# A hybrid encoder block on one core: the SwiGLU down projection as seven products behind all gate and up blocks

## The chip, the cores and the metric

The kernel runs on one core of a Trainium2 chip. The engines named below are TensorE (PE; its weight loads are shown apart as PEld), VectorE (DVE), ScalarE (ACT), GpSimd (POOL) and SyncE (SP, which only issues transfers here). The metric is the device time of one execution in microseconds, as the median over several executions.

## The reference

One layer is applied to a prompt of 256 tokens and a sample of 512 tokens, 768 tokens together, with a model width of 1024. It holds an RMSNorm, a joint input projection, three token mixers (a bidirectional state-space scan, a differential attention, an attention into 256 memory tokens), a gated merge with an output projection, and a SwiGLU FFN. The change concerns the FFN, whose hidden width D_FF is 2816. All arrays are float32.

```python
D_FF = -(-8 * D_MODEL // (3 * 256)) * 256
...
    merged = jnp.sum(gates * br.astype(F32), axis=2).astype(x.dtype)
    x = x + merged @ w_out[li]

    h2 = rmsnorm(x, ffn_norm_g[li])
    g, up = jnp.split(h2 @ w_gate_up[li], 2, axis=-1)
    x = x + (jax.nn.silu(g) * up) @ w_down[li]
    return x
```

## The kernel before

**Products in three passes.** A float32 product is made of three matmuls on float32r parts: each operand is split into a high part (a ScalarE copy that rounds) and a low part (the difference, on VectorE, or by an adding transfer on POOL's queue). `mm3` issues high x high, high x low, low x high into one PSUM tile. `split_evac` makes such a pair.

**Weights.** `WStream` holds a list of weight blocks, filled by `W.add` in the order of use. A block is loaded in two halves of 128 x 1024 from SP's queue into the pool "wr" (3 buffers), and split into "wh" and "wl" (4 buffers of 128 x 1024 each, line 544). `W.get` hands out the next block and starts the one behind it (`ahead`, line 605). A block of kind "w" is cut into seven factors of 128 x 512: three are quarters of the block (wh_A, wl_A), the others come from sums and differences that POOL makes in the pool "ws" (line 563 on). A block of kind "x" takes its first half from two extra tiles, so that it rotates with the others.

**The FFN.** The 2816 hidden features are 11 blocks of 256. The normed input lies in F, features on partitions, as a high and a low part of 128 x 8 x 768. Block 0 is computed plainly: `first` makes one gate or up tile of 128 features and 256 or 512 tokens from 24 matmuls. For blocks 1 to 10 gate and up are each a product by Strassen's scheme in Winograd's form: `block` (line 1453) cuts the weights, the features and the tokens in halves and makes seven products of 12 matmuls (128 x 384), where the plain one takes eight. The right factors are quarters B11 to B22 of F and T1 to T4, sums of them, which `right_factors` makes once on VectorE and ScalarE, in steps that end with a `yield`; T4 overwrites B12. The code runs these steps between the tiles of block 0 by calls of `next(factors)`. Within `block`, `plus` adds the products up in two tiles of the pool "brr" (2 buffers), and `fin_gate` (tanh on ScalarE, then VectorE) and `fin_up` (a multiply on POOL) put the result into `act_in`, 128 x 2 x 768. `fin_up` then splits it into hidh (ScalarE) and hidl (VectorE).

**Down.** `down(fb)` (line 1487) takes block fb's 256 hidden features at once: for each of six token tiles and two halves of the 1024 output columns, six matmuls of 128 x 512 go into a PSUM tile, and VectorE adds it into the residual `x1`. The last call also stores the outputs. The order is written by hand (line 720): gate 0, up 0, down 0, gate 1, up 1, and then gate fb, down fb - 1, up fb.

**Who sets the order.** The program is put in order by a scheduler that simulates the engines' times; within an engine or a queue it then runs in that order. So the order of the code is a priority, and an instruction whose inputs or buffers are free sooner can go ahead of one that stands before it in the code. Tiles in pools are reused when their last reader is done.

**Memory around the FFN.** Before the FFN, three branches are projected. In `tail` (line 1552), ahead of the last quarter of the first branch, the pools of the differential attention are closed, their memory becomes XB (48 KB a partition), and eight chunks of z are loaded from DRAM on POOL's queue and split into the pair Z that the next product reads. Four of the chunks go through "zst" (3 buffers), the others through "brr". XB later holds F.

Of the kernel before, what the change touches and what calls it, by code (L numbers as in the profile page):

```python
# [486 lines left out]
TOK = 768  # L487
# [16 lines left out]
class WStream:  # L504
# [7 lines left out]
    def __init__(self, nc, tc, ctx):  # L512
        self.nc = nc
        self.praw = ctx.enter_context(tc.tile_pool(name="wraw", bufs=3))
        self.ph = ctx.enter_context(tc.tile_pool(name="whi", bufs=4))
        self.pl = ctx.enter_context(tc.tile_pool(name="wlo", bufs=4))
        self.sub = nc.vector
        self.by_dma = False
        self.extra = None
# [23 lines left out]

    def _tile(self, i, extra=False):
        ph, pl = self.extra if extra else (self.ph, self.pl)
        return (ph.tile([128, self.HALF], F32R, name=f"wh{i}", tag="wh"),
                pl.tile([128, self.HALF], F32R, name=f"wl{i}", tag="wl"))

    def _factor(self, i, key, src):

        if self.half is None:
            t, sl = self._tile(f"{i}_{key}"), slice(0, 512)
# [6 lines left out]
        self.nc.scalar.activation(f(hi), src, AF.Copy)  # L559
        self.nc.vector.tensor_tensor(out=f(lo), in0=src, in1=f(hi).bitcast(F32), op=ALU.subtract)  # L560
        self.parts.setdefault(i, {})[key] = f(hi), f(lo)
# [23 lines left out]
    def _split(self):  # L585
# [3 lines left out]
        if kind == "w":  # L589
            return self._split_w(i, h)  # L590
        hi, lo = self._tile(f"{i}_{h}", kind == "x" and h == 0)
        self.parts.setdefault(i, []).append((hi, lo))
# [36 lines left out]
def hybrid_block(ctx, tc, A, outs, consts):  # L629
# [89 lines left out]
    wd = A["w_down"].rearrange("(k p) c -> p k c", p=128)  # L719
    order = [("gate", 0), ("up", 0), ("down", 0), ("gate", 1), ("up", 1)]  # L720
    for fb in range(2, NFB):
        order += [("gate", fb), ("down", fb - 1), ("up", fb)]
    order.append(("down", NFB - 1))
    for what, fb in order:
        if what == "down":
            W.add(wd[:, 2 * fb : 2 * fb + 2, :], 2, 1024, "x")
        else:
            W.add(cols("w_gate_up", 256 * fb + (DFF if what == "up" else 0)), 8, 256, "w" if fb else None)

# [25 lines left out]

    def mm3(ps, wh, wl, xh, xl, start, stop):
        pe.matmul(ps, wh, xh, start=start, stop=False)  # L757
        pe.matmul(ps, wh, xl, start=False, stop=False)  # L758
        pe.matmul(ps, wl, xh, start=False, stop=stop)  # L759

# [74 lines left out]
    z_scr = [dr.tile([128, TOK], F32, name=f"z_scr{m}") for m in range(8)]  # L835
    gl_scr = [dr.tile([128, TOK], F32, name=f"gl_scr{m}") for m in range(24)]
    br_scr = [dr.tile([128, TOK], F32, name=f"br_scr{m}") for m in range(8)]
    mo_scr = [dr.tile([128, 8, TOK], F32, name=f"mo_scr{w}") for w in "hl"]
# [287 lines left out]

    x1ctx, dctx, wctx = ExitStack(), ExitStack(), ExitStack()
    stg = x1ctx.enter_context(tc.tile_pool(name="stg", bufs=2))
# [287 lines left out]
    HT = TOK // 2  # L1416
    hid = {}
    act_in = {}
# [7 lines left out]
    def fin_up(fb, c, m, cs, eng=v):  # L1426
        hh, hl = hid[fb]
        o = act_in[fb][:, m, cs]
        eng.tensor_tensor(out=o, in0=o, in1=c, op=mul)
        act.activation(hh[:, m, cs], o, AF.Copy, scale=0.5)  # L1430
        v.scalar_tensor_tensor(out=hl[:, m, cs], in0=o, scalar=0.5, in1=hh[:, m, cs].bitcast(F32),
                               op0=mul, op1=sub)

    def new_block(what, fb):
        if what == "gate":
            act_in[fb] = fa.tile([128, 2, TOK], F32, name=uid("fa"), tag="fa")
        else:
            hid[fb] = tuple(fh.tile([128, 2, TOK], F32R, name=uid("hid" + w), tag="hid" + w) for w in "hl")

# [12 lines left out]

    def block(what, fb):

# [17 lines left out]
        kw = {} if what == "gate" else {"eng": gp}  # L1472
        act.activation(c12, prod("A11", "B11"), AF.Copy)
        plus(c11, c12, prod("A12", "B21"))
        fin(fb, c11, 0, h1, **kw)
# [9 lines left out]
        fin(fb, c21, 1, h1, **kw)  # L1485

    def down(fb, last):
        w = W.get()
        x = hid.pop(fb)
        for tt in (3, 4, 5, 0, 1, 2) if fb else range(TILES):  # L1490
            for c0 in (0, 512):
                ps = (psd if c0 else env.psb)("dn")
                dense_tm(ps, w, c0, 512, x, tt, 2)
                o = x1[tt][:, c0 : c0 + 512]
                v.tensor_tensor(out=o, in0=o, in1=ps, op=add)  # L1495
                if last:
                    nc.sync.dma_start(os_[tt][:, c0 : c0 + 512], o)


    with ExitStack() as c5:  # L1500
# [51 lines left out]
        def tail(c):  # L1552
# [3 lines left out]
            dctx.close()  # L1556
            L["XB"] = x1ctx.enter_context(tc.tile_pool(name="XB", bufs=1))
# [3 lines left out]
            xp = x1ctx.enter_context(tc.tile_pool(name="x1", bufs=1))  # L1561
            L["x1"] = [xp.tile([128, 1024], F32, name=f"x1_{t}") for t in range(TILES)]

# [30 lines left out]
        c6 = ctx.enter_context(ExitStack())  # L1594
        fa = c6.enter_context(tc.tile_pool(name="ffa", bufs=1))
        ft_ = c6.enter_context(tc.tile_pool(name="fft", bufs=2))
# [54 lines left out]

    W.extra = tuple(c6.enter_context(tc.tile_pool(name="wx" + w, bufs=1)) for w in "hl")
    W.sums = c6.enter_context(tc.tile_pool(name="wsum", bufs=3))
    tp = c6.enter_context(tc.tile_pool(name="ffT", bufs=1))
    fh = c6.enter_context(tc.tile_pool(name="ffh", bufs=1))

# [4 lines left out]
    def right_factors():  # L1661

        with tc.tile_pool(name="ffb", bufs=1, side="right") as p:
# [29 lines left out]
            b21 = whole(t1, "B21")  # L1693
            v.tensor_tensor(out=b21, in0=b21, in1=t2, op=sub)
            R["T4"] = B["B12"]
            split_evac(*R["T4"], b21)
# [4 lines left out]
    for sg, m in ((0, 0), (0, 1), (1, 0), (1, 1)):  # L1701
        for what in ("gate", "up"):
            if sg or what == "up":
                first(what, sg, m)
                if sg and m + (what == "up"):
                    next(factors)
    down(0, False)
    next(factors)
    next(factors, None)
    for what, fb in order[3:]:  # L1710
        if what == "down":
            down(fb, fb == NFB - 1)
        else:
            block(what, fb)
    c6.close()
    x1ctx.close()

# [42 lines left out]
```

## Time and profile before

| | |
|---|---|
| median of 3 executions | 1789.56 us (1787.43 to 1792.11) |
| span of the profiled execution, first to last instruction | 1787.8 us |
| mean granted TensorE clock | 0.999 |
| PE, PEld, DVE busy | 99%, 91%, 73% |
| ACT, POOL busy | 48%, 15% |
| moved by DMA in the span | 205.25 MB |
| start of the first down matmul, start of the last addition | 1287.8 us, 1783.9 us |

The profile names the execution's span but no other time of it; the table has the executions beside it. A line of a group of instructions reads: line of the kernel, engine, operation, tiles written and read, shape, count, then busy time and mean duration, then the idle time of the engine ahead of the group with what ended it. A line of the timeline begins with the start and the duration in us. Tile names in the FFN: "gate" and "up" are PSUM tiles of the blocks, "dn" those of the down projection, "fs" the sums of `block`, "fa" is `act_in`, "ft" the tanh, "wr" a raw weight, "wh" and "wl" its parts, "ws" POOL's sums.

### The profile page before, as it was taken

The numbers are of one execution on the slowest core, as the hardware profiler recorded it, in microseconds if no ns is written. First come the engines' busy times: TensorE is split into PE (matmuls) and PEld (weight loads), VectorE is DVE, ScalarE is ACT, GpSimd is POOL, SyncE is SP. The second block draws the span as 40 slices with busy tenths as digits, with TensorE's granted clock in tenths as the row PEclk, the third lists the DMA queues.
The fourth block names the chain that finished last, engine by engine and source line by source line (L and its number), as shares of the span: only waits on it lengthen the run. The fifth ranks groups of instructions, "written<-read, shape, count | busy, mean of one in ns | idle before, by whom it ended". The sixth has DMA issues, their size and how long they took to land.

```text
span 1787.8 us, 29382 instructions
## 1 busy us (share of the span) xinstructions
PE 1761.9 (99%) x11293; PEld 1624.4 (91%) x11293; DVE 1301.2 (73%) x2411; ACT 861.7 (48%) x1838; POOL 261.8 (15%) x276
## 2 busy tenths in 40 slices
PE   9999999999999999999989999999999999999999
PEld 8999988999999999999979888888889999999997
DVE  6665659699999589778865545452699777877775
ACT  6444434777676356777756433232333333333331
POOL 0000000000000101011110101000115333333330
PEclk9999999999999999999999999999999999999999
DMA  7223645664656466553862635332312222222221
GB/s 264 72 83 107 133 118 127 160 147 126 157 146 152 122 164 152 112 113 82 188 166 71 219 116 171 115 98 68 83 48 71 72 71 71 71 71 71 71 71 71
DMA packets 193196, 205.25 MB, mean 115 GB/s; under 512 B 56856, under 2 KB 166688, under 8 KB 193056
## 3 DMA queue, kind: packets, MB, share of 16 engines
q1 hardware_dynamic: 173632, 146.74, 28.0%
q0 software_dynamic: 18272, 53.48, 13.6%
q10 hardware_dynamic: 1152, 3.15, 0.5%
q8 instruction: 89, 1.46, 0.3%
q14 instruction: 51, 0.42, 0.1%
HBM read 145.59 MB, written 32.57 MB: 100 GB/s over the span
## 4 chain that ended last, share of the span: by engine, by line
PE 57%; DVE 4%; DMA 2%; issue 1%; ACT 1%; POOL 0%; SPq 0%; DVEq 0%; ACTq 0%; POOLq 0%
PE br L757 4%; PE br L758 4%; PE br L759 4%; PE dn L757 3%; PE dn L758 3%; PE dn L759 3%; PE gate L757 3%; PE gate L759 3%; PE gate L758 3%; PE up L757 3%; PE up L759 3%; PE up L758 3%; PE av L1316 2%; PE qk L758 2%; PE qk L757 2%; PE qk L759 2%
## 5 line engine op out<-in xcount | busy, mean ns | idle before, releaser
L597 ACT ACTIVATE wh<-wr 128x1024 fp32r<-128x1024 f32 x146 | 163.7, 1122 | 106.6 <-PE br L758 27.0
L603 DVE TENSOR_TENSOR wl<-wr,wh 128x1024 fp32r<-128x1024 f32 x104 | 135.2, 1302 | 102.1 <-ACT wh L597 100.3
L757 PE MATMUL gl<-Hhi,wh 128*128 128x256 f32 (+1 forms) x384 | 132.4, 345 | 2.3 <-ACT glt L1119 2.3
L1495 DVE TENSOR_TENSOR x<-x,dn 128x512 f32<-128x512 f32 x132 | 88.7, 684 | 56.5 <-PE dn L759 56.1
L759 PE MATMUL gl<-Hhi,wl 128*128 128x256 f32 (+1 forms) x384 | 129.0, 336 | 0.0
L758 PE MATMUL gl<-Hlo,wh 128*128 128x256 f32 (+1 forms) x384 | 128.7, 335 | 0.0
L757 PE MATMUL qk<-wh,Hhi 128*128 128x256 f32 x384 | 108.1, 281 | 0.7 <-ACT V L1215 0.7
L758 PE MATMUL qk<-wl,Hhi 128*128 128x256 f32 x384 | 108.6, 283 | 0.0
L759 PE MATMUL qk<-wh,Hlo 128*128 128x256 f32 x384 | 107.9, 281 | 0.0
L559 ACT ACTIVATE wh_S<-ws 128x512 fp32r<-128x512 f32 x70 | 41.7, 623 | 130.1 <-PE dn L759 103.5
L757 PE MATMUL dn<-wh,hidh 128*128 128x512 f32 x264 | 102.4, 390 | 1.3 <-DVE x L1495 1.0
L601 POOL DMA_DIRECT2D wl<-wr x42 | 36.8, 876 | 454.0 <-ACT wl L600 430.5
L758 PE MATMUL dn<-wl,hidh 128*128 128x512 f32 x264 | 102.9, 390 | 0.0
L759 PE MATMUL dn<-wh,hidl 128*128 128x512 f32 x264 | 100.8, 390 | 0.0
L757 PEld LDWEIGHTS gl<-Hhi,wh 128*128 128x128 f32 x384 | 72.3, 188 | 9.7 <-ACT glt L1119 2.7
L759 PEld LDWEIGHTS gl<-Hhi,wl 128*128 128x128 f32 x384 | 72.0, 188 | 8.1
L758 PEld LDWEIGHTS gl<-Hlo,wh 128*128 128x128 f32 x384 | 72.2, 188 | 7.2
L1285 DVE TENSOR_REDUCE nm<-sc 128x1 f32<-128x512 f32 (+1 forms) x96 | 56.5, 597 | 28.0 <-PE sc L1280 27.0
L757 PEld LDWEIGHTS qk<-wh,Hhi 128*128 128x128 f32 x384 | 72.4, 188 | 1.6 <-ACT V L1215 0.9
L759 PEld LDWEIGHTS qk<-wh,Hlo 128*128 128x128 f32 x384 | 72.8, 190 | 0.3
L758 PEld LDWEIGHTS qk<-wl,Hhi 128*128 128x128 f32 x384 | 72.2, 188 | 0.6
L1287 ACT ACTIVATE p<-sc,nm 128x512 f32<-128x512 f32 (+1 forms) x96 | 59.1, 619 | 17.0 <-DVE nm L1285 16.6
(466 smaller groups left out, 5927.6 us busy)
## 6 DMA issues: line engine op xcount, KB each, us to landing
wr<-in_w_in_dram SPq DMA_DIRECT2D x48, 512.0 KB, 4.6
wr<-in_w_gate_up_dram SPq DMA_DIRECT2D x44, 512.0 KB, 3.5
wl<-wr POOLq DMA_DIRECT2D x42, 512.0 KB, 5.3
wr<-in_w_branch_dram SPq DMA_DIRECT2D x24, 512.0 KB, 4.2
wr<-in_w_down_dram SPq DMA_DIRECT2D x22, 512.0 KB, 4.2
glr<-gl_scr POOLq DMA_DIRECT2D x24, 384.0 KB, 3.7
wr<-in_w_mem_kv_dram SPq DMA_DIRECT2D x16, 512.0 KB, 3.7
wr<-in_w_in_dram SPq DMA_DIRECT2D x32, 256.0 KB, 4.5
```

What stands on the lines that cost most here:

```text
L559: self.nc.scalar.activation(f(hi), src, AF.Copy)
L597: self.nc.scalar.activation(hi, r, AF.Copy)
L601: self.nc.gpsimd.dma_start(lo, r.bitcast(F32R), accum_op=ALU.add)
L603: self.sub.tensor_tensor(out=lo, in0=r, in1=hi.bitcast(F32), op=ALU.subtract)
L757: pe.matmul(ps, wh, xh, start=start, stop=False)
L758: pe.matmul(ps, wh, xl, start=False, stop=False)
L759: pe.matmul(ps, wl, xh, start=False, stop=stop)
L1285: v.tensor_reduce(out=nm[:, m : m + 1], in_=ps, axis=AX.X, op=ALU.max, negate=True)
L1287: act.activation(pm[:, 0:n], ps, AF.Exp, bias=nm[:, m : m + 1], accum_out=s1s[:, tt : tt + 1] if m == 0 else s2)
L1316: pe.matmul(po[:, 0:128], aT[:, 128 * k : 128 * k + 128], V[:, c0 // 128 + k, 128 * (h % 2) : 128 * (h % 2) + 128], start=(k == 0), stop=( ...
L1495: v.tensor_tensor(out=o, in0=o, in1=ps, op=add)
```

## The change

The down projection isn't done block by block any more. All gate and up blocks run first, gate and up in turns; each finished `act_in` block (no longer split) is stored to a DRAM tensor, `hid_scr`, from SP's queue (`hid_store`). Then the whole product of 768 tokens x 2816 features x 1024 columns is made with tokens, features and columns cut in halves, as seven products of 384 x 1408 x 512 in the same scheme as gate and up (P1, P5, P6, P3, P7, P2, P4 in this order). A product runs over 11 chunks of 128 features in six granules (five of two chunks, one of one); a granule is 18 matmuls of 128 x 512, three token tiles in three PSUM tiles. Products that belong together are summed in PSUM without being read out in between, in two groups of banks ("b" and "d") used in turns; behind every product VectorE adds three PSUM tiles into `x1`, or subtracts them.

The left operands are sums and differences of quarters of the activations, loaded back from DRAM once each (24 loads, on SP) and combined in place on VectorE, then split. The right operands are sums of quarters of `w_down`, made by transfers: a plain load on SP's queue, then an adding one on POOL's queue onto the same tile (P5, P6, P4 on six tiles "ch", P7 on raw buffers). Loads are issued four granules ahead and operands made two ahead. Three granules' activations and weights are fetched in the middle of the last up block (`hook`).

Beside that: `act_in` has two buffers instead of one, the extra weight tiles and the hid tiles go, `x1` is allocated ahead of XB so that XB can be closed after the gate and up blocks, "zst" has two buffers instead of three, and the steps of `right_factors` are called after each up tile and each gate tile but the last pair, with one more `yield`.

```diff
-    order = [("gate", 0), ("up", 0), ("down", 0), ("gate", 1), ("up", 1)]
-    for fb in range(2, NFB):
-        order += [("gate", fb), ("down", fb - 1), ("up", fb)]
-    order.append(("down", NFB - 1))
+    order = [(what, fb) for fb in range(NFB) for what in ("gate", "up")]
...
     def fin_up(fb, c, m, cs, eng=v):
-        hh, hl = hid[fb]
         o = act_in[fb][:, m, cs]
         eng.tensor_tensor(out=o, in0=o, in1=c, op=mul)
-        act.activation(hh[:, m, cs], o, AF.Copy, scale=0.5)
-        v.scalar_tensor_tensor(out=hl[:, m, cs], in0=o, scalar=0.5, in1=hh[:, m, cs].bitcast(F32),
-                               op0=mul, op1=sub)
+
+    def hid_store(fb):
+        nc.sync.dma_start(hid_scr[:, 2 * fb : 2 * fb + 2, :], act_in.pop(fb))
...
-        zst = zctx.enter_context(tc.tile_pool(name="zst", bufs=3, side="right"))
+        zst = zctx.enter_context(tc.tile_pool(name="zst", bufs=2, side="right"))
...
-                if sg and m + (what == "up"):
+                if (sg, m) != (1, 1):
                     next(factors)
-    down(0, False)
-    next(factors)
-    next(factors, None)
-    for what, fb in order[3:]:
-        if what == "down":
-            down(fb, fb == NFB - 1)
+    for _ in factors:
+        pass
+    hid_store(0)
...
+    P1, P5, P6, P3, P7, P2, P4 = range(7)
+    GRAN = [(k, min(2, NFB - k)) for k in range(0, NFB, 2)]
+    NG = len(GRAN)
+    ITEMS = [(p, g) for p in range(7) for g in range(NG)]
+    AHEAD, FETCH = 2, 4
+    EARLY = 3
...
+    def a_load(q, g):
+        k0, n = GRAN[g]
+        r, kh = q
+        early = q == (0, 0) and g < EARLY
+        t = (da_e if early else DP["a"]).tile([128, 2, HT], F32, name=f"da{r}{kh}_{g}")[:, 0:n]
+        nc.sync.dma_start(t, hid_scr[:, NFB * kh + k0 : NFB * kh + k0 + n, HT * r : HT * r + HT])
+        a_raw[q, g] = t
...
+    def w_fetch(i):
...
+        if p in (P5, P6, P4):
+            if p == P5:
+                ch[g] = view(DP["ch"].tile([128, 1024], F32, name=f"dch{g}"))
+                nc.sync.dma_start(ch[g], w_quarter(0, 0, g))
+            t = ch[g]
+            src, acc = None, {P5: (0, 1), P6: (1, 1), P4: (1, 0)}[p]
         else:
-            block(what, fb)
+            t = view(W.praw.tile([128, W.HALF], F32, name=f"dwr{i}", tag="wr"))
+            src, acc = {P1: ((0, 0), None), P3: ((1, 1), None), P7: ((0, 1), (1, 1)), P2: ((1, 0), None)}[p]
+            nc.sync.dma_start(t, w_quarter(*src, g))
+        if acc:
+            gp.dma_start(t, w_quarter(*acc, g), accum_op=add)
+        w_raw[i] = t
...
+    def make(i):
...
+        split_evac(wh, wl, t)
...
+        xh, xl = (da_f.tile([128, 2, HT], F32R, name=uid("dx" + w), tag="dx" + w)[:, 0:n] for w in "hl")
+        split_evac(xh, xl, x, sign)
+        parts[i] = xh, xl, wh, wl
+
+    def down_early():
+        for i in range(FETCH - 1):
+            w_fetch(i)
+        for g in range(EARLY):
+            a_load((0, 0), g)
+        for i in range(AHEAD):
+            make(i)
+
+    for what, fb in order[2:]:
+        block(what, fb, down_early if (what, fb) == order[-1] else None)
+        if what == "up":
+            hid_store(fb)
     c6.close()
+    xbctx.close()
...
+        loads = [((0, 0), g) for g in range(EARLY, NG)]
+        loads += [(q, g) for g in range(NG) for q in ((1, 0), (1, 1))] + [((0, 1), g) for g in range(NG)]
...
+        for _ in range(NG - EARLY):
+            a_load(*loads.pop(0))
+        w_fetch(FETCH - 1)
+        for i, (p, g) in enumerate(ITEMS):
+            for _ in range(3):
+                if loads:
+                    a_load(*loads.pop(0))
+            w_fetch(i + FETCH)
+            make(i + AHEAD)
+            bank = "b" if p in (P1, P6, P7, P4) else "d"
...
+            for t in range(3):
+                c = slice(128 * t, 128 * t + 128)
+                for k in range(n):
+                    mm3(ps[t], xh[:, k, c], xl[:, k, c], wh[:, k], wl[:, k],
+                        g == 0 and k == 0 and p in (P1, P5, P2), g == NG - 1 and k == n - 1, p in (P6, P3, P7, P4))
+            if g == NG - 1:
+                r, f, op = HOME[p]
+                for t in range(3):
+                    o = x1[3 * r + t][:, 512 * f : 512 * f + 512]
+                    v.tensor_tensor(out=o, in0=o, in1=ps[t], op=op)
+                    if p in (P3, P7, P2, P4):
+                        nc.sync.dma_start(os_[3 * r + t][:, 512 * f : 512 * f + 512], o)
```

More of the change, by code (lines that the diff above doesn't have):

```diff
@@ L1451, in first, with block @@
         (fin_gate if what == "gate" else fin_up)(0, ps[:, 0:n], m, slice(c0, c0 + n))
-    def block(what, fb):
+    def block(what, fb, hook=None):
         new_block(what, fb)
@@ new lines, in make @@
+    def make(i):
+        if i >= len(ITEMS):
+            return
+        p, g = ITEMS[i]
+        n = GRAN[g][1]
+        t = w_raw.pop(i)
+        wh, wl = (x.rearrange("p (k c) -> p k c", k=2)[:, 0:n] for x in W.tiles(f"d{i}"))
+        split_evac(wh, wl, t)
+        A_ = lambda r, kh: a_raw[(r, kh), g]
+        tt = lambda o, x, y, op: v.tensor_tensor(out=o, in0=x, in1=y, op=op)
+        sign = 0.5
+        s_ = None if p == P1 else A_(1, 0)
+        if p == P1:
+            x = A_(0, 0)
+        elif p == P5:
+            x = s_
+            tt(x, x, A_(1, 1), sub)
+        elif p == P6:
+            x = s_
+            tt(x, x, A_(0, 0), sub)
+        elif p == P3:
+            x = DP["t"].tile([128, 2, HT], F32, name=uid("ds4"), tag="ds4")[:, 0:n]
+            tt(x, s_, A_(0, 1), add)
+        elif p == P7:
+            x = s_
+            tt(x, x, A_(1, 1), add)
+            sign = -0.5
+        else:
+            x = A_(*((0, 1) if p == P2 else (1, 1)))
+        xh, xl = (da_f.tile([128, 2, HT], F32R, name=uid("dx" + w), tag="dx" + w)[:, 0:n] for w in "hl")
+        split_evac(xh, xl, x, sign)
+        parts[i] = xh, xl, wh, wl
```

80 lines of the change are left out of this document (44 added, 36 removed).

## The prediction

> **What bounds the kernel now.** I read first the page's totals, then the chain that ended last, then the gate, up and down stages of the FFN one by one, then its start, then the transfers.
>
> ```profile
> span 1787.8 us, 29382 instructions
> PE 1761.9 (99%) x11293; PEld 1624.4 (91%) x11293; DVE 1301.2 (73%) x2411; ACT 861.7 (48%) x1838; POOL 261.8 (15%) x276
> 1783.68 0.24 PE dn L759
> 1783.94 0.69 DVE x L1495
> ```
>
> TensorE (PE) is busy 99% of the span, and the chain runs through its down-projection matmuls ("dn") up to the last at 1783.68; one addition and the store follow, 4.1 us to the end. A change in FFN time is therefore a change in TensorE's work or in its waits. There are 11 blocks x 6 token tiles x 2 column halves x 2 chunks x 3 passes = 792 dn matmuls. Their duration of 0.39 us isn't their price, because they overlap. The next rows (start, duration) give the pitch: the first of one down stage, the first behind it, and the first of the gate block after that.
>
> ```profile
> 1371.91 0.39 PE L757 MATMUL dn<-wh,hidh 128*128 128x512 f32 x1
> 1388.27 0.33 PE L757 MATMUL up<-fhi,wh_A 128*128 128x384 f32 x1
> 1402.85 0.33 PE L757 MATMUL gate<-fhi,wh_A 128*128 128x384 f32 x1
> ```
>
> 72 matmuls took 1388.27 - 1371.91 = 16.36 us, so one costs 0.227 us. The 84 of an up block take 1402.85 - 1388.27 = 14.58 us. Stage by stage (columns: window, length, then busy time of PE, weight load, DVE, ACT, POOL with counts, clock, DMA share, GB/s):
>
> ```profile
> 1357.40:1371.90 14.50, 14.50 (x85) 14.50 (x84) 14.19 (x20) 6.70 (x12) 8.43 (x6) 1.00 0.32 97
> 1371.90:1388.30 16.40, 16.40 (x74) 13.55 (x74) 11.69 (x18) 1.74 (x4) 4.78 (x3) 1.00 0.03 11
> ```
>
> TensorE doesn't stop in either stage, but VectorE (DVE) is 98% busy in the gate stage. The down stage is where it catches up.
>
> **The change, part by part.** My sum starts from the span of the profiled execution, 1787.8 us; the median of the runs, 1789.56, lies 1.8 above it, and I carry the difference over to the median.
>
> (1) Matmuls. Seven products x 3 token tiles x 11 feature chunks x 3 passes = 693 instead of 792, of the same shape. 99 x 0.227 = **-22.5 us**. (By durations it would be 38.6, which is wrong for overlapping matmuls.)
>
> (2) Additions into x1: 132 of 0.69 us become 21. They were beside TensorE but for 1.2 us of waits ("dn" 1.0, "gate" 0.2), which go: **-1.2**.
>
> ```profile
> PE dn L757 <- DVE x L1495: 1.0, 1, 1.0
> PE gate L757 <- DVE x L1495: 0.2, 1, 0.2
> ```
>
> (3) Start of the FFN. Down block 0 used to stand between the first gate/up pair and gate block 1, and it covered the making of the factors T1 to T4 on VectorE.
>
> ```profile
> 1287.80:1305.00 17.20, 17.20 (x77) 14.25 (x76) 7.42 (x8) 2.50 (x4) 4.59 (x3) 1.00 0.00 1
> 1305.00:1322.40 17.40, 17.25 (x77) 13.94 (x76) 17.40 (x21) 8.10 (x12) 5.58 (x3) 1.00 0.20 61
> 1322.40:1343.50 21.10, 20.05 (x110) 19.15 (x111) 21.10 (x26) 7.56 (x12) 4.16 (x3) 1.00 0.15 50
> 1343.50:1357.40 13.90, 12.89 (x74) 12.41 (x73) 13.90 (x20) 6.85 (x14) 7.49 (x5) 1.00 0.39 114
> 1327.07 1.75 DVE L751 TENSOR_TENSOR T2l<-fB,T2h 128x1536 fp32r<-128x1536 f32 x1
> ```
>
> VectorE is full from 1305 to 1357, but idles 17.20 - 7.42 = 9.8 us before that. The moved next(factors) calls start T1 right after the first up tile, so that idle time can be used. Gate block 1 needs T2 for its third product: 1287.8 + 20.8 (the rest of block 0, 22.2 less 1.4 of dn) + 4.2 (two products) = 1312.8. T2 was ready at 1327.07 + 1.75 = 1328.8. About 3.2 us of down work ahead of it on VectorE goes, and 9.8 us of idling may: 1315.8, 3 us late. If none of the idling is used it is 13 late; if the order helps, 0. T4 writes into B12 and must follow the last up tile, as before it followed down 0; it is needed 12 us later still. I take **+4**, between 0 and 13.
>
> (4) Gate and up back to back, ten pairs. One old period (gate, down, up, from 1403 on; 45.4 us) by groups on VectorE (count | busy, mean ns | idle before):
>
> ```profile
> L1495 DVE TENSOR_TENSOR x<-x,dn 128x512 f32<-128x512 f32 x12 | 8.1, 685 | 5.8 <-PE dn L759 5.8
> L560 DVE TENSOR_TENSOR wl_S<-ws,wh_S 128x512 fp32r<-128x512 f32 x7 | 5.6, 821 | 0.0
> L560 DVE TENSOR_TENSOR wl_A<-wr,wh_A 128x512 fp32r<-128x512 f32 x5 | 5.0, 1024 | 1.1 <-ACT wh_A L559 1.1
> L1424 DVE SCALAR_TENSOR_TENSOR fa<-ft,fs 128x384 f32<-128x384 f32 x4 | 4.4, 1104 | 0.2
> L1467 DVE TENSOR_TENSOR fs<-fs,up 128x384 f32<-128x384 f32 x8 | 4.3, 545 | 0.4 <-PE up L759 0.4
> L1467 DVE TENSOR_TENSOR fs<-fs,gate 128x384 f32<-128x384 f32 x7 | 3.7, 545 | 0.0
> L603 DVE TENSOR_TENSOR wl<-wr,wh 128x1024 fp32r<-128x1024 f32 x2 | 2.5, 1225 | 2.1 <-ACT wh L597 2.1
> L1431 DVE SCALAR_TENSOR_TENSOR hidl<-fa,hidh 128x384 fp32r<-128x384 f32 x4 | 2.1, 548 | 0.0
> L560 DVE TENSOR_TENSOR wl_A<-ws,wh_A 128x512 fp32r<-128x512 f32 x1 | 1.5, 1544 | 0.1
> L560 DVE TENSOR_TENSOR wl_S<-wr,wh_S 128x512 fp32r<-128x512 f32 x1 | 0.7, 685 | 0.0
> ```
>
> All ten sum to 37.9. Additions (8.1), the down weights' low parts (2.5) and hidl (2.1) leave the stage: 25.2 us remain, against 29.1 of TensorE. It fits, at 87%, without the cover that the down stage gave. The price of a failure lies in the spread of durations (ns min/median/max):
>
> ```profile
> L560 DVE TENSOR_TENSOR wl_S<-ws,wh_S x70: 676/685/1773, 1309.9 to 1754.3; 128x512 fp32r<-128x512 f32 x70
> L1467 DVE TENSOR_TENSOR fs<-fs,gate x63: 540/544/556, 1363.3 to 1738.9; 128x384 f32<-128x384 f32 x63
> L579 POOL TENSOR_TENSOR ws<-wr x20: 1292/1710/1742, 1291.2 to 1731.2; 128x512 f32<-128x512 f32 x20
> ```
>
> An operation with both inputs in SBUF (wl_S) can take 1.1 us longer, while one that reads PSUM (fs) never does. A pair has 12 POOL operations. If each delayed one on VectorE by 1.1, the undelayed time (14 x 0.685 + 14 x 0.545, and 4 of fs's size, so 19.4) becomes 32.6, 3.5 over TensorE's 29.1: 35 us in ten pairs. Lower bound 0; I take **+1**, by the 25.2. The Trainium skill, GPSIMD Engine Reference, section Specifications, says that GpSimd's SBUF interfaces are shared with VectorE and contend with its instructions that have two SBUF inputs. The trace agrees (685 against 1773 ns, and no spread at fs); it is the mechanism of the rival below.
>
> POOL keeps its work (17 of now 29 us). The hidden blocks' 11 stores go to SP's queue behind up's last multiply; queued there are weight loads for a block that begins about 14 us later, so they cost nothing as long as that lead holds, a few us if it is gone.
>
> (5) Loads of the down stage. From the end of the last up block to product 5's fourth granule, the code's order moves 7.47 MB of activations, 1.31 MB of product 1's weights, 2.10 MB of first addends and 2.10 MB of added ones: 12.98 MB.
>
> ```profile
> q1 hardware_dynamic: 173632, 146.74, 28.0%
> GB/s 0 26 189 284 364 405 376 381 408 398 357 262 356 415 414 383 364 347 341 218 24 0 233 233 250 252 269 284 277 288 357 408 349 88 4 0 88 300 337 193
> wr<-in_w_down_dram SPq DMA_DIRECT2D x22, 512.0 KB, 4.2
> wl<-wr POOLq DMA_DIRECT2D x42, 512.0 KB, 5.3
> L601 POOL DMA_DIRECT2D wl<-wr x42 | 36.8, 876 | 454.0 <-ACT wl L600 430.5
> L753 ACT ACTIVATE zhi<-brr x8: 838/842/848, 1000.2 to 1009.2; 128x768 fp32r<-128x768 f32 x8
> L754 DVE SCALAR_TENSOR_TENSOR zlo<-brr,zhi x8: 949/951/959, 1001.1 to 1010.0; 128x768 fp32r<-128x768 f32 x8
> ```
>
> In the first 45 us (second row) full queues reached about 400 GB/s; SP's queue averaged 146.74 MB in 28.0% of the span, 293 GB/s. That makes 32 to 44 us, plus 5.2: 2.9 of latency (4.2 of landing less 0.52 MB at 400 GB/s), 1.1 for the weights' high part (zhi's 0.84 for 768 columns, scaled to 1024) and 1.2 for the low one (L603): 38 to 50. It is due after product 1 (99 x 0.227 = 22.5) and three granules (18 x 0.227 = 4.1 each): 34.8. So 3 to 15 us late in the code's order, and 0 if the weight loads, whose buffers come free sooner, are issued ahead. I take **+3**. The Trainium skill, DMA: Bandwidth & Descriptors, section Specifications, gives about 358 GB/s of HBM per core; by it 12.98 MB take 36.3 us and the delay is 6.7. The windows above 400 speak against it as a limit here.
>
> (6) Product 7 loads and then adds into three raw buffers: 4.2 + 0.9 (POOL's issue) + 5.3 + 1.1 + 1.2 = 12.7 us a turn, 4.2 an item against 4.1: **+1.5**, 0 to 4. VectorE has per item 1.2 (weights' low part), twice 0.95 (the activations' low part and a sum, at zlo's size) and 0.4 of additions (21 x 0.685 over 38.5 full items): 3.5 of 4.1, hidden.
>
> (7) zst shrinks from 3 buffers to 2. Z's fifth chunk then waits for the third's low part.
>
> ```profile
> 1001.78 0.51 PE L757 MATMUL glu<-zhi,wh 128*128 128x256 f32 x2
> 1002.58 3.56 DVE L754 SCALAR_TENSOR_TENSOR zlo<-brr,zhi 128x768 fp32r<-128x768 f32 x4
> 1002.35 0.54 POOL L1545 DMA_DIRECT2D brr<-z_scr  x1 [18.17 <-DVE zlo L754]
> DMA to landing us min/median/max: 3.4/4.3/4.4
> ```
>
> Today the first load to wait for such a buffer goes out at 1002.35, behind the first chunk. The third chunk ends near 1004.4 (it is the second of the four in 3.56 us); issue 0.5, landing 4.3, zhi 0.84 make 1010.0. TensorE runs out of the four chunks that it has at 1007.4 (from 1001.8; three PSUM tiles, of 256, 512 and 256 columns, make 9 matmuls or 1.4 us a chunk): **+2.6**, 0 to 4.
>
> Sum: -22.5 - 1.2 + 4 + 1 + 3 + 1.5 + 2.6 = -11.6, span 1776.2, median **1778.0**. The tail of 4.1 us stays: the last product ends in the same addition and store.
>
> **The rivals.** *All of it hidden*: VectorE uses its 9.8 idle us, and weight loads go out early. For it: the quoted idle time, and a DMA share of 0.32 in a gate stage. Against: (7) has a computed gap. 1789.6 - 23.7 = 1766. *Loads starve product 5*: 15 instead of 3, 1790, no change. For: 12.98 MB in 34.8 us are 373 GB/s, against 97 in a gate stage today; against: the code's order isn't binding. *The factors come late*: 13 instead of 4, 1787. For: VectorE was full for 52 us there. *VectorE and POOL bound the ten pairs*: 1778 + 34 = 1812, slower. For: 98% in the gate stage; against: 25.2 < 29.1. It decides once a pair takes over 30.9 us, 1.8 above 29.1, as ten times 1.8 eat the 11.6 and (with +1 already in) 5.4 more.
>
> **How the numbers follow.** Forecast 0.41, all hidden 0.21, loads 0.13, factors 0.10, VectorE and POOL 0.15. 0.3% (5.4 us) is about what a measurement of this kernel tells from no change: 1784.2 to 1795. Faster: 0.38 + 0.21 + 0.04 = 0.63; same: 0.03 + 0.08 + 0.07 = 0.18; slower 0.19. The forecast's own range is 1770 to 1786; with all hidden below and loads or factors plus a little more above, 1764 to 1797.
>
> **What would show it.** 693 matmuls of the down stage at 0.227 (157.5 us); gate and up in 29.1 us per pair without PE gaps; PE's waits near 1310 (T2), near 1007 (zhi), and at product 5's start on "ch" transfers. VectorE over 95% in the pairs with PE waiting for its sums, or a down stage over 175 us, would make it wrong.

## The result, and the profile after

The change made the kernel slower: 1802.01 us, median of four executions (1798.56 to 1804.47), against 1789.05 in four of the kernel before beside them. The ratio is 1.0069, 95% interval 1.0053 to 1.0085. The prediction was 1778.0, in a range of 1764 to 1797. The profiled execution of the new kernel spans 1801.5 us, 13.7 more than before's 1787.8. Its page has (totals, then two transfer queues with packets, MB and share of 16 engines' span):

```profile
span 1801.5 us, 29429 instructions
PE 1751.7 (97%) x11194; PEld 1611.7 (89%) x11194; DVE 1263.3 (70%) x2342; ACT 886.6 (49%) x1856; POOL 281.4 (16%) x300
q1 hardware_dynamic: 185584, 166.93, 30.5%
q0 software_dynamic: 24288, 65.02, 16.9%
```

TensorE is busy for 97% instead of 99%: it has 10 us less to do and stands still for longer. The view of its waits (total in us, times, longest in us) has two large ones that before does not have:

```profile
PE dn L751 <- ACT dxh L745: 17.3, 2, 16.6
PE glu L751 <- ACT zhi L745: 8.7, 1, 8.7
```

Where the 13.7 us are is read from five starts in the timeline of TensorE. Before, the first gate tile and gate block 2:

```profile
1270.95 0.40 PE L757 MATMUL gate<-fhi,wh 128*128 128x256 f32 x2
1357.35 0.33 PE L757 MATMUL gate<-fhi,wh_A 128*128 128x384 f32 x1
```

After, the same two, the first down matmul and the last:

```profile
1281.63 0.40 PE L751 MATMUL gate<-fhi,wh 128*128 128x256 f32 x2
1351.18 0.33 PE L751 MATMUL gate<-fhi,wh_A 128*128 128x384 f32 x1
1613.27 0.39 PE L751 MATMUL dn<-whd,dxh 128*128 128x512 f32 x1
1797.36 0.40 PE L753 MATMUL dn<-whd,dxl 128*128 128x512 f32 x1
```

- Up to the FFN: 1281.63 - 1270.95 = **+10.7**. The wait for z is 8.7 of it. Behind it, from 1014.0 to 1021.5, the granted clock is 0.55 and TensorE is busy for 5.0 us, so about 5.0 x 0.45 = 2.3 more are lost (an estimate).
- The FFN's start: 69.55 us against 86.40, which held down block 0 (16.36): **-0.5**.
- Nine gate and up pairs: 262.09 us, 29.12 each, against 45.4 - 16.36 = 29.04: **+0.7**.
- All down work, tail included: 1801.5 - 1613.27 = 188.2 us. Before, what is left of the span is 1787.8 - 1357.35 - 9 x 29.04 + 16.36 = 185.4: **+2.8** instead of -22.5.

The four make 13.7. In the down stage all of the 22.5 us and a little more are given back by the wait of 16.6, by smaller waits (1.4), by a clock of 0.58 behind the long wait (3.1) and by a matmul every 0.2334 us instead of 0.227 (4.4).

The wait of 16.6, in the timeline of SP's and POOL's queues (start, duration):

```profile
1609.30 3.49 SPq L1725 DMA_DIRECT2D dch<-in_w_down_dram  x6
1612.88 3.13 SPq L1731 DMA_DIRECT2D dwr<-in_w_down_dram  x2
1615.12 1.22 POOL L1733 DMA_DIRECT2D dch<-in_w_down_dram  x1 [3.58 <-ACT whd L742]
1617.64 1.95 POOL L1422 TENSOR_TENSOR fa<-fa,fs 128x384 f32<-128x384 f32 x1
1618.60 5.56 POOL L1733 DMA_DIRECT2D dch<-in_w_down_dram  x4
1619.62 0.33 SPq L1425 DMA_DIRECT2D hid_scr<-fa  x1
1629.90 28.70 SPq L1708 DMA_DIRECT2D da<-hid_scr  x21
```

Product 5's weights, plain and adding, are issued before the last hidden block is stored. That store is issued 6.4 us behind the last up matmul and needs 10.2 us to land while the DMA engines are full. The 21 activation loads wait for it: their buffers lie over its source. Product 1 has three granules' activations and stops at the fourth. Four windows (start and end, length, busy PE, PEld, DVE, ACT, POOL, clock, DMA share, GB/s):

```profile
1613.30:1626.00 12.70, 12.70 (x55) 9.88 (x53) 4.40 (x4) 2.74 (x3) 9.04 (x8) 1.00 1.03 319
1626.00:1642.60 16.60, 0.03 (x1) 0.00 (x0) 1.23 (x2) 1.90 (x2) 1.20 (x1) 0.57 1.10 257
1642.60:1650.00 7.40, 7.39 (x20) 5.81 (x21) 2.55 (x4) 1.36 (x2) 0.00 (x0) 0.58 1.08 315
1650.00:1665.00 15.00, 15.00 (x66) 12.10 (x65) 13.84 (x16) 7.76 (x9) 2.39 (x2) 1.00 1.07 345
```

The DMA engines are full throughout, but at the smallest rate while TensorE stands still. The queues of the window 1600 to 1650 say why (MB and share):

```profile
q1 hardware_dynamic: 5185, 9.62, 55.9%
q0 software_dynamic: 1776, 3.41, 36.9%
```

SP's plain transfers moved 9.62 MB in 0.559 x 50 = 27.95 us of the engines, 344 GB/s. POOL's adding ones moved 3.41 MB in 18.45 us: **185 GB/s**, about half the rate. It isn't POOL's queue as such that is slow: from 996 to 1012 of the same execution it carried x1 and z without adding, 3.74 MB in 64.2% of 16 us, which is 364 GB/s.

The other wait, near 1005, in the timelines of POOL and ScalarE after:

```profile
998.50 1.06 POOL L1563 DMA_DIRECT2D x<-in_x_prompt_dram  x2 [14.10 <-ACT do L1334]
999.55 2.09 POOL L1563 DMA_DIRECT2D x<-in_x_sample_dram  x4
1001.63 1.08 POOL L1525 DMA_DIRECT2D brr<-z_scr  x2
1004.07 0.54 POOL L1525 DMA_DIRECT2D brr<-z_scr  x1 [1.37 <-DMA x<-in_x_prompt_dram]
1013.18 0.84 ACT L745 ACTIVATE zhi<-brr 128x768 fp32r<-128x768 f32 x1 [9.80 <-DMA brr<-z_scr]
```

and of POOL before:

```profile
1004.70 0.54 POOL L1545 DMA_DIRECT2D brr<-z_scr  x1 [0.33 <-DVE zlo L754]
1011.59 1.06 POOL L1583 DMA_DIRECT2D x<-in_x_prompt_dram  x2 [0.71 <-DVE zlo L754]
```

The six loads of the residual x1, 13 us earlier than before, stand ahead of z's on POOL's queue, and ScalarE waits 9.80 us for z. The first loads of z go out no later than before (1001.63 against 1002.35); what is late is their landing, behind 3.1 MB of x1: a median of 11.5 us for four of them, against 4.3 for three of before's.

### The profile page after: what moved, and what is told of

It is laid out like the page before. It is cut to its first block, busy times and chain, and to the rows that moved or that the text cites. A ratio compares the mean times of both kernels' runs of the same rounds, so it can differ in the third digit from the quotient of the medians.

```text
span 1801.5 us, 29429 instructions
## 1 busy us (share of the span) xinstructions
PE 1751.7 (97%) x11194; PEld 1611.7 (89%) x11194; DVE 1263.3 (70%) x2342; ACT 886.6 (49%) x1856; POOL 281.4 (16%) x300
## 3 DMA queue, kind: packets, MB, share of 16 engines
q10 hardware_dynamic: 1152, 3.15, 0.5%
## 4 chain that ended last, share of the span: by engine, by line
PE 52%; DMA 5%; DVE 4%; issue 2%; ACT 1%; POOL 0%; SPq 0%; DVEq 0%; ACTq 0%; POOLq 0%
PE br L752 4%; PE br L751 4%; PE br L753 3%; PE up L751 3%; PE up L752 3%; PE up L753 3%; PE gate L751 3%; PE gate L753 3%; PE gate L752 3%; PE dn L751 2%; PE dn L753 2%; PE dn L752 2%; PE av L1311 2%; PE qk L752 2%; PE qk L751 2%
## 5 line engine op out<-in xcount | busy, mean ns | idle before, releaser
L595 ACT ACTIVATE wh<-wr 128x1024 fp32r<-128x1024 f32 x124 | 140.4, 1133 | 63.3 <-PE br L752 18.1
L601 DVE TENSOR_TENSOR wl<-wr,wh 128x1024 fp32r<-128x1024 f32 x82 | 108.3, 1324 | 81.3 <-ACT wh L595 79.4
L751 PE MATMUL dn<-whd,dxh 128*128 128x512 f32 x231 | 92.5, 402 | 17.3 <-ACT dxh L745 17.3
L752 PE MATMUL dn<-wld,dxh 128*128 128x512 f32 x231 | 92.4, 401 | 0.1
L753 PE MATMUL dn<-whd,dxl 128*128 128x512 f32 x231 | 89.8, 400 | 0.7 <-DVE dxl L746 0.7
L751 PEld LDWEIGHTS dn<-whd,dxh 128*128 128x128 f32 x231 | 44.1, 191 | 29.0 <-ACT dxh L745 18.5
L558 DVE TENSOR_TENSOR wl_S<-ws,wh_S 128x512 fp32r<-128x512 f32 x70 | 57.8, 849 | 15.2 <-ACT wh_S L557 15.2
```

Source lines behind the costliest of these rows:

```text
L595: self.nc.scalar.activation(hi, r, AF.Copy)
L601: self.sub.tensor_tensor(out=lo, in0=r, in1=hi.bitcast(F32), op=ALU.subtract)
L751: pe.matmul(ps, wh, xh, start=start, stop=False, **kw)
L752: pe.matmul(ps, wh, xl, start=False, stop=False, **kw)
L753: pe.matmul(ps, wl, xh, start=False, stop=stop, **kw)
```

## The experiments

Times are medians in us; a ratio, with its 95% interval, is to the kernel before on the same chip, whose median lay between 1791.03 and 1792.04 in these runs, some 2 to 3 us above the 1789.05 further up. Where nothing else is said, a kernel is the changed one with the edit shown.

**Was it zst, or x1's new place in memory?** e1 is the kernel before with one digit changed.

```diff
-        zst = zctx.enter_context(tc.tile_pool(name="zst", bufs=3, side="right"))
+        zst = zctx.enter_context(tc.tile_pool(name="zst", bufs=2, side="right"))
```

> The kernel before, with the pool zst cut from 3 to 2 buffers and nothing else. Theory A (the cut lets the six loads of x1, 3.1 MB, go ahead of the last four loads of z on POOL's queue, and the glu products wait for z): the whole loss of the changed kernel at 1002 to 1016 us appears here too, +8 to +12 us over before, with the x1 loads issued before 1002 us and one TensorE wait of 7 to 9 us for zhi. Rival A1 (x1's place in memory, ahead of XB, is what lets its loads go early): no such order here, +0 to +4 us.

1802.86, ratio 1.0062 (1.0047 to 1.0077). The buffer alone costs as much as the 10.7 us above (1802.86 against 1791.85); x1's place was not changed here.

```profile
PE glu L757 <- ACT zhi L753: 8.2, 1, 8.2
999.40 1.06 POOL L1583 DMA_DIRECT2D x<-in_x_prompt_dram  x2 [14.01 <-ACT do L1339]
1002.53 1.08 POOL L1545 DMA_DIRECT2D brr<-z_scr  x2
```

In these rows (a wait, two of POOL's timeline) x1's loads overtake z's here too. e2 keeps two buffers and forbids that.

```diff
-            gp.dma_start(zs, z_scr[M])
+            zs_i = gp.dma_start(zs, z_scr[M])
+            if M == 1:
+                zs_last = zs_i.ins
...
-        for t in range(TILES):
-            gp.dma_start(x1[t], xs[t])
+        with tc.issue_after(zs_last):
+            for t in range(TILES):
+                gp.dma_start(x1[t], xs[t])
```

> The changed kernel with the loads of x1 held behind the second load of zs on POOL's queue; zst stays at 2 buffers. Theory A (the order of the loads costs it, not the count of buffers as such): -7 to -11 us against the changed kernel, some 1791 to 1795 us, TensorE's wait for zhi down from 8.7 to 0 to 3 us. Rival A2 (a z chunk that waits for a free buffer is late anyway): -0 to -4 us, the wait stays over 5 us.

1794.04, ratio 1.0014 (1.0005 to 1.0024); the wait of glu is 0.5 us. So what costs is not the third buffer itself but the order that the scheduler chose with two. e5 to e13, but for e11, keep this edit.

**The wait in product 1.** e3 gives 16 activation tiles a pool that lies on memory free before the last store.

```diff
-        t = (da_e if early else DP["a"]).tile([128, 2, HT], F32, name=f"da{r}{kh}_{g}")[:, 0:n]
+        pool = da_e if early else DP["a" if len(a_raw) < EARLY + 16 else "a2"]
+        t = pool.tile([128, 2, HT], F32, name=f"da{r}{kh}_{g}")[:, 0:n]
...
-        for k, n in (("a", 1), ("ch", 1), ("t", 2)):
+        for k, n in (("a", 1), ("a2", 1), ("ch", 1), ("t", 2)):
```

> The changed kernel with the pool of the activations' quarters cut in two, so that its first 16 tiles lie on XB's 48 KB alone and the rest over the memory of the gate and up blocks' buffers. Theory B (the loads wait for the store of the last hidden block, whose source lies under the one large pool): the first of these loads is issued within 3 us of the last up matmul instead of 16.6 us behind it, TensorE's wait of 16.6 us in product 1 falls under 5 us, the clock stays up; -14 to -20 us, some 1782 to 1788 us. Rival B1 (the DMA engines are full from the up block's end on, so an earlier issue doesn't land earlier): the wait stays over 8 us there or comes back at product 5; -0 to -8 us.

1809.9, ratio 1.0095 (1.0078 to 1.0112).

```profile
PE dn L751 <- ACT dxh L745: 16.3, 5, 8.6
```

The loads do go out earlier now, the first at 1617.2, but one wait of 16.6 became five of 16.3 in sum. So the place decides where TensorE waits, and hardly how long in all. The ratio is above the changed kernel's 1.0069, which neither theory had: from its first matmul to its last the down stage takes 188.1 us instead of 184.1, with a clock of 0.83 from 1640 to 1660 and of 0.80 from 1660 to 1680, behind several waits instead of one. e5 takes work off the engines: product 5's adding transfers are left out, and with them the second quarter of the weights.

```diff
-        if acc:
+        if acc and p != P5:
             gp.dma_start(t, w_quarter(*acc, g), accum_op=add)
```

> The changed kernel with the x1 loads behind z (as in e2_x1_behind_z), and without the six adding transfers of product 5: the second quarter of the weights is not added there, nor is it in what products 6 and 4 build on those tiles. In product 1 TensorE waits 16.3 to 16.6 us, while the adding transfers and plain loads keep the DMA engines at 99% or more and only some 250 GB/s get through. Theory F (the adding transfers take the DMA engines' time that the activations need): the store of the last block of hid lands in 5 us or less instead of 10.2, the activations of granule 3 in 7 us or less instead of 11.7, the wait in product 1 falls to 4 to 8 us, the idle clock loss with it, and the time is 8 to 12 us below e2's 1794.0, at 1782 to 1786. Rival G (the place of the activations under the last block's source sets the wait, whatever else is in the queues): the chain store, load, split keeps its length to within 2 us, the wait stays at 14 us or more, and the time is 1790 or more.

1777.72, ratio 0.9917 (0.9902 to 0.9933), 16.3 us below e2. A wait, and two pieces of the chain:

```profile
PE dn L751 <- ACT dxh L745: 2.7, 1, 2.7
1608.28 8.01 DMA hid_scr<-fa
1617.28 3.68 DMA da<-hid_scr
```

The wait goes, as theory F has it and rival G does not; the gain is larger than theory F's range (1782 to 1786). The 2.88 MB of addends cost 15.6 us at 185 GB/s, close to what came back, but the two need not be the same thing: the store still took 8.0 and not 5 us, and it was issued 1.9 us behind the last up matmul (1606.36) and not 6.4, because POOL's last multiplies no longer stand among the issues of adding transfers. So e5 shows what these transfers cost as a whole; it does not part their rate from their place on POOL's queue.

**Can order hide them?** e9 holds each of those transfers until its granule's activations have landed; e6 does this with e3's pools and holds the later products' raw weights back too. (Both also carry e8's shift, below.)

```diff
+        if acc and p == P5:
+            x = a_raw[(1, 1), g]
+            seen = sm.tile([128, 2], F32, name=uid("seen"), tag="seen", bufs=4)
+            i_ = gp.tensor_tensor(out=seen, in0=x[:, 0, 0:2], in1=x[:, 0, 2:4], op=add)
+            with tc.issue_after(i_.ins):
+                gp.dma_start(t, w_quarter(*acc, g), accum_op=add)
-        if acc:
+        elif acc:
```

> As e8_dx_shift, and each adding transfer of product 5 waits until the activations of its own granule have landed; the activations' buffers stay in one pool, under the last block's source. Theory F: with the adding transfers out of the way the store of the last block lands in 6 us or less and the wait in product 1 falls from 16.3 to 5 to 9 us; what is pushed back may cost up to 5 us in product 5; 1778 to 1786. Rival G: the wait stays at 14 us or more and the time is at e8's or above.

> The changed kernel with every cost found so far taken out by order and place: x1's loads behind z; the activations' buffers in two pools, so that 16 of them lie on what is free before the last block's store; each adding transfer of product 5 held until the activations of its own granule have landed (a GpSimd addition of 128 x 2 elements reads them first); the raw weights of the later products held behind the last of those loads; and the split activations shifted by 64 bytes (see e8_dx_shift). If order and the DMA engines' time are the whole cause: no wait over 2 us in the down stage, pitch 0.2267, 1794.0 - 16.3 - 3 - 4.6 = about 1770, with 1768 to 1778 for what is left over; that is faster than before by 0.8 to 1.3%. If the DMA engines cannot carry 12.98 MB in this stretch in any order (rival), the waits come back in products 5 and 6 as they did in e3_split_pool, with 10 us or more in all, and the time is 1780 to 1795.

e9: 1803.58, ratio 1.0062 (1.0046 to 1.0077). e6: 1797.66, ratio 1.0034 (1.0019 to 1.0048). e9's wait in product 1 falls to 2.7 us, below the 5 to 9 of theory F, but product 5 pays 17.8 us instead of up to 5. e6 has none in product 1, and waits for product 5's weights:

```profile
PE dn L752 <- DVE wld L743: 11.1, 1, 11.1
PE dn L751 <- ACT whd L742: 3.1, 1, 3.1
```

The rival is right on the waits: these bytes, at this rate, did not fit between the up blocks and product 5 in either order. A part of both results is something else: with the small tiles "seen" the operands' addresses differ from e8's (table below), and both reach the down stage 3.5 to 3.6 us later than e8. That is more than the 2.7 us by which e6 lies above its rival's range.

**The pitch.** e4 exchanges the two inner loops, so that successive triples go to another PSUM tile.

```diff
-            for t in range(3):
-                c = slice(128 * t, 128 * t + 128)
-                for k in range(n):
+            for k in range(n):
+                for t in range(3):
+                    c = slice(128 * t, 128 * t + 128)
```

> The changed kernel with the loops over token tiles and over the two feature chunks of a granule exchanged, so that nine matmuls read the same weight chunk in a row instead of three. The down matmuls of the changed kernel start 0.2333 us apart, those of the kernel before 0.2267. Theory C (the pitch goes with how often the moving operand changes between the halves of a weight tile): about 0.227 to 0.230 here, some 2 to 4 us less in sum. Rival C1 (it goes with something else: the stationary operand's place, the sum in PSUM that is never restarted): 0.233 as before.

1802.54 in one execution; the pitch stays 0.2334. e8 moves the split activations by 64 bytes.

```diff
+    de.enter_context(tc.tile_pool(name="pad", bufs=1, side="right")).tile([128, 16], F32, name="pad16")
     da_f = de.enter_context(tc.tile_pool(name="daf", bufs=3, side="right"))
```

> The changed kernel with the x1 loads behind z and one unused tile of 64 bytes ahead of the split activations of the down projection, so that their addresses, which are the stationary operand of its matmuls, are 32 and no longer 96 modulo 128 bytes. Two groups of 128x128 by 512 matmuls issue every 0.2333 us, the down projection after the change and the output projection wo in both kernels, and in the program both have their stationary operand at 96 modulo 128, while all groups at 0.2267 to 0.228 have it at 32. Theory C2 (the address of the stationary operand sets the pitch): the down projection's pitch falls to 0.227 and wo's stays at 0.2333; 693 x 0.0066 = 4.6 us less than e2, of which a part can go into the wait in product 1: 1789 to 1791. Rival C3 (a sum kept over many groups in PSUM, which wo and the down projection also share, sets it): pitch stays 0.2333, time 1794.

1792.9, ratio 1.0002 (0.9992 to 1.0012); the profiled span is 1789.6 against e2's 1792.2. The median is 1.1 us below e2's and above the 1789 to 1791 expected. Two rows of TensorE's timeline, after, ten matmuls apart (2.34 us):

```profile
1668.14 0.40 PE L752 MATMUL dn<-wld,dxh 128*128 128x512 f32 x1
...
1670.48 0.40 PE L752 MATMUL dn<-wld,dxh 128*128 128x512 f32 x1
```

and in e8, sixteen apart (3.63 us):

```profile
1690.15 0.39 PE L751 MATMUL dn<-whd,dxh 128*128 128x512 f32 x1
...
1693.78 0.39 PE L752 MATMUL dn<-wld,dxh 128*128 128x512 f32 x1
```

That is 0.234 against 0.227, with the same instructions and wo still at 0.2333. The address moved the pitch; of the 4.4 us, longer waits (17.8 against 16.3) took back 1.5. But "32 modulo 128 is fast" was the wrong rule: in e6 and e9 the stationary operand has that, and dn takes 0.2324. What fits the runs measured is the distance between the two operands. e11 tests it on the kernel before, with 64 bytes ahead of the weights' buffers.

```diff
     sm = ctx.enter_context(tc.tile_pool(name="small", bufs=4))
+    sm.tile([128, 16], F32, name="pad16", bufs=1)
```

> The kernel before with one unused tile of 64 bytes ahead of the weights' buffers, nothing else. Over after, e6 and e8 a single rule fits the pitch of all 512-wide groups: slow (0.2327 to 0.2363) where the address of the stationary operand less that of the moving one is 64 or 128 modulo 256 bytes, fast (0.2267 to 0.229) where it is 0 or 192. Here wo goes from 64 to 0, gl and br from 192 to 0, and glu and the down projection stay at 0. By the rule wo's 288 matmuls fall from 0.2333 to 0.227 (-1.9 us) and no other 512-wide group changes: 1789 to 1791 on this chip's 1792. If instead the address of the stationary operand alone decides (which e6 speaks against), wo keeps 0.2333.

1795.51, ratio 1.0022 (1.0011 to 1.0032). The mean distance of successive starts, over stretches of the timeline without a gap or a missing record, against the address of the stationary operand less that of the moving one, modulo 256 bytes (the addresses are those of the built programs):

| group, width | kernel | distance | us a matmul |
|---|---|---|---|
| dn, 512 | before; e8 | 0 | 0.2272; 0.2271 |
| wo, 512 | e11 | 0 | 0.2268 |
| gl, 512 | e11; before | 0; 192 | 0.2277; 0.2291 |
| wo, 512 | e6 | 192 | 0.2289 |
| dn, 512 | e6 | 128 | 0.2324 |
| dn; wo, 512 | after | 64 | 0.2335; 0.2333 |
| gl, 512 | e6 | 64 | 0.2333 |
| qk, 256 | before; e6; e11 | 64; 192; 0 | 0.1179; 0.1206; 0.1212 |
| v, 256 | before; e6; e11 | 64; 192; 0 | 0.1166; 0.1190; 0.1212 |

By the rule wo had to fall, and it did: 288 x 0.0065 = 1.9 us. That the time rose is in the last two rows: for groups 256 wide the distance 64 is the fast one. The 1152 matmuls of qk lose 1152 x 0.0033 = 3.8 us and the 576 of v 576 x 0.0046 = 2.6; the sum of the three is 4.5, and the median rose by 4.5, though other groups moved too. The expectation that only 512-wide groups would change was wrong.

**A way round the adding transfers.** In e10, e12 and e13 product 5's addend is loaded plainly on SP and added by GpSimd; all three have 64 bytes of shift, e10 and e12 ahead of the weights' buffers, where it costs the 256-wide groups time as in e11, and e13 ahead of the split activations, as e8. e12 and e13 also hold the later products' loads back. The diff is a part of e12's; `seen[(1, 1), g]` is the load of that granule's activations (in e10 of granule 3 or 5).

```diff
+        if acc and p == P5:
+            b = view(DP["b"].tile([128, 1024], F32, name=uid("dcb"), tag="cb"))
+            with tc.issue_after(seen[(1, 1), g]):
+                nc.sync.dma_start(b, w_quarter(*acc, g))
+            gp.tensor_tensor(out=t, in0=t, in1=b, op=add)
-        if acc:
+        elif acc:
```

> The changed kernel with the x1 loads behind z, a 64-byte tile ahead of the weights' buffers, and the addend of product 5's weights loaded plainly into a buffer of its own behind the loads of granules 3 and 5 of activations, and added by GpSimd (six additions of 128 x 1024) instead of by the DMA engines. e5 without these additions stood at 1777.7 with 2.7 us of waits in the down stage; the addends are 2.88 MB, which is 16.6 us at the 174 GB/s that the adding transfers reached and 8.7 us at the 332 GB/s of the plain loads. Theory F2 (the price is the slow rate of adding transfers): 0 to 9 us of waits come back instead of 16, and the pitch of 0.227 takes 4.6 us away (see e11): 1774 to 1783, faster than before by 0.5 to 1.0%. Rival H (the engines are short of time for any second operand here): waits of 14 us or more, 1786 to 1792.

> As e10_plain_addend, and the activations' buffers in two pools, so that the first 16 loads need not wait for the last block's store; behind them on SP's queue come the addends, and behind those the activations of product 3 and the raw weights of products 3, 7 and 2. If the engines' time is what is left, and what is needed first comes first: the 2.7 us wait of product 1 goes, and no wait over 2 us comes in product 5: 1770 to 1776, the fastest so far. If the bytes cannot be carried in time, the waits stand in product 5 instead: 1778 to 1786.

> As e12_plain_ordered, with the addend of product 5's granule g loaded right behind the two activations of that granule, so that GpSimd's additions start in product 1, and with the 64-byte tile ahead of the split activations (as in e8_dx_shift) and not ahead of the weights' buffers, where it cost the 256-wide groups 0.12 instead of 0.117 us a matmul. e12's profile has 9.9 us of waits at the start of product 5 and a clock of 0.50 to 0.62 behind them (about 3 us), because the first addend landed at 1631; it reaches the end of the gate and up blocks 1.8 us later than e8. If order is all that was left: waits below 3 us in the whole down stage, 1785.5 - 9.9 - 3 - 1.8 = 1771 for the span, 1771 to 1776 on the median, faster than before by 0.9 to 1.1%. If GpSimd's additions, at 2.8 us each beside a busy VectorE, set the pace of product 5 instead: waits of 5 us or more remain there, 1777 to 1783.

e10: 1798.88, ratio 1.0045 (1.0032 to 1.0058): a miss, with 18.8 us of waits in the down stage, since the addends stood last in the queue. e12: 1788.29, ratio 0.9978 (0.9967 to 0.9989): product 1 has no wait, product 5 has 9.9 us, outside what either theory had. e13: 1785.56, ratio 0.9964 (0.9950 to 0.9977), the fastest that computes the whole layer, but not the 1771 to 1776 of its theory. Its waits, the group of GpSimd's additions (ns min/median/max), and an operation of VectorE in the timeline:

```profile
PE dn L752 <- DVE wld L743: 5.5, 3, 3.3
PE dn L751 <- ACT whd L742: 3.3, 1, 3.3
L1745 POOL TENSOR_TENSOR dch<-dch,dcb x6: 2249/2496/6822, 1624.1 to 1654.0; 128x1024 f32<-128x1024 f32 x5, 128x512 f32<-128x512 f32 x1
1633.78 3.99 DVE L1760 TENSOR_TENSOR da<-da,da 128x768 f32<-128x768 f32 x1
```

8.8 us of waits remain in product 5, where an addition took up to 6.8 us and an operation of VectorE beside one 3.99 instead of 0.94: its rival, though 2.6 us above the range that it gave. So the same bytes with plain transfers, reordered, ended about 7 us below e8, which has the same shift (ratios 0.9964 and 1.0002). Order and kind were changed together here; e6 and e9 show that order alone did not do it. Additions on VectorE were not tried.

## Why the prediction was wrong, step by step

The sign that the prediction gave for being wrong did come: a down stage of over 175 us. It took 1797.36 - 1613.27 = 184.1 from its first matmul to its last. Two terms make up nearly all of the miss, (5) and (7); (1) adds to it, and (3) takes some off.

- **(1) Matmuls, -22.5.** The count was right, the pitch was not: 693 x (0.2334 - 0.227) = 4.4 us less of a gain. "Of the same shape" was taken to mean "of the same pitch". wo, of that shape and at 0.2333, stood in before's trace.
- **(2) Additions, -1.2.** Right: neither of the two waits is left.
- **(3) FFN start, +4.** Right in mechanism, too dear: -0.5. VectorE's idle time took up the delay: T2 was ready at 1321.0, 39.4 us behind the first gate tile, and the prediction's count needed it 41.9 us behind.
- **(4) Gate and up back to back, +1.** Right: 29.12 us a pair. VectorE and POOL did not become the bound, so the rival with the highest price falls.
- **(5) Loads of the down stage, +3.** The step that failed most: 16.6 + 3.1 us, in product 1 and not in product 5. All bytes were divided by one range of rates, 293 to 400 GB/s, while the adding transfers went at 185; without product 5's the time falls by 16.3 us (e5). The clock behind a wait was not priced at all. A due time was worked out for product 5's weights alone, not for the activations behind the last block's store, and the scheduler had put product 5's weights ahead of that store. The sentence on weight loads "issued ahead" named this hoisting and counted it as a help.
- **(6) Product 7, +1.5.** 1.4 us of small waits, between 1738 and 1746: right. There the chain runs through a load into a raw buffer (dwr), as predicted.
- **(7) zst, +2.6.** Right place and same buffer, wrong size: 10.7. The sum counted the wait of a chunk for its buffer. It left out who else was on POOL's queue: x1's loads went first, and z's landed behind them (e1, e2). It also left out the halved clock behind the wait. x1's new place in memory, e1's rival, was no cause.

On the Trainium skill's figure, about 358 GB/s of HBM per core (DMA: Bandwidth & Descriptors, Specifications), which stood beside step 5: the fullest 6 us of e13 (1618 to 1624, DMA share 1.04) moved 403 GB/s. No run here shows it as a limit.

## What to carry to other kernels

Price transfers by kind before adding up bytes, and give every load on a shared queue its own due time; a scheduler fills a blocked queue with whatever is ready, and that is what the next stage then stands behind. When a buffer is taken from a loader, list what else its queue holds. In a window at 100% DMA share, order alone did not take the waits away here (e6, e9); fewer transfers (e5) or another kind of them (e12, e13) did.

## What the hardware showed that was not expected

- Adding transfers from DRAM took nearly twice the engines' time of plain ones: 185 against 344 GB/s in one window, and 364 for plain ones on the same queue as the adding ones.
- 64 bytes of address changed a matmul's pitch by up to 4% (v, 0.1166 to 0.1212), in opposite directions for 512 and 256 moving columns (table above). Why was not found.
- Behind a wait of 16.6 us, 20 matmuls took 7.4 us at a granted clock of 0.58. The Trainium skill, TensorE: Matmul & The Clock Gate, Part 1, has the clock halved after an idle window of about 3.4 us and back after a busy one as long, and these windows running freely. The halving agrees. The way back had no fixed length: in e4 the 7.4 us behind a wait of 15.8 us had a clock of 0.78, and 25 matmuls started in them.
- GpSimd's additions of 128 x 1024 and VectorE's of 128 x 768 took 2.4 to 6.8 us and 0.94 to 3.99 us in e13; the longest of both fell where the two ran side by side.
